# One order for all engines of the wide SwiGLU, worked out in the source; h^T copied back to SBUF; four of eight K pairs of gate and up summed

## The chip, the cores and the metric

The kernel runs on one core of a Trainium2 chip. The metric is the device time of one execution in microseconds, as a median of runs. The core has TensorE (PE, its weight loads shown apart as PEld), VectorE (DVE), ScalarE (ACT), GpSimd (POOL) and SyncE (SP), each with an instruction queue of its own that is worked off in order.

## The reference

One layer of an encoder for 256 tokens of width 2048: two attention branches with a common output projection, a cross-attention, then a SwiGLU feed-forward network, and a last normalization. All is float32. The change touches the feed-forward network (FFN_HIDDEN is 5632):

```python
hf = rms_norm(x, g_ffn[layer])
x = x + (jax.nn.silu(hf @ w_gate[layer]) * (hf @ w_up[layer])) @ w_down[layer]
```

and, in the order of the matmuls alone, the output projection of the attention (w_out).

## The kernel before

**Products.** TensorE works in fp32r, so each operand is split into a high and a low part, and each product is three matmuls (`mm`, L99 to L101): activations high by weights high, high by low, low by high. The activations (names ending in _h, _l, 128x128) are the stationary side, the weights (wh, wl, 512 columns) the moving one. `split_into` makes the parts: ACT casts the high one (L107), DVE subtracts it from the source for the low one (L108). Weights come from DRAM raw (wraw, three buffers of 128x2048, one DMA for each on SP's queue), and are split into four buffers of wh and wl.

**Stages of the FFN.** 5632 hidden columns are one narrow chunk of 512 (`narrow_chunk`, weights w_gate0 and w_up0, input x2T) and five wide ones of 1024 (`wide_chunk`, input xn). While the narrow chunk runs, `normalized_pairs` makes xn: x2T_f is multiplied by the row of 1/rms (rrow), and split. A wide chunk is a projection by gate, a silu on ACT, a projection by up, the product h = u g on DVE, and the transposes of h (`pt`, L502) for w_down. The narrow chunk and the first wide one make the first group, the other four two groups of two. Behind each group, its part of w_down is added to x_res (`wide_add`) in two halves of 1024 columns; the accumulators start from x_res, copied in by ACT (L261).

**Pairs.** The 2048 rows of a projection's weights are 8 K pairs of 256. A plain pair (P) takes 8 products, 24 matmuls. A summed one (W) takes 7 products in the manner of Strassen and Winograd, 21 matmuls, for which DVE makes sums of the weights (`tsum`, L287 to L292) and, once for each activation pair, sums of the activations (`sums`, L245 to L248, and their split, `forms`). The W pairs of a projection gather four of their products in the accumulators q1, q5, q7 and q6; `leave` (L332 to L336) turns these into four partial results on ACT and DVE, and `join` (L340) adds the accumulators of the plain products. `GU_KINDS` gives the kind of each pair, `G_ORDER` and `U_ORDER` the order in which gate and up take them; `DN_KINDS` and `groups` do so for w_down.

**What sets the order.** In the kernel before, the order of the instructions on each engine comes from the scheduler of the language: the code is written stage by stage, and the scheduler interleaves what stands open, by its own estimate. The buffers (three of wraw, four of wh and wl, eight PSUM banks, in two pools that change roles from one projection to the next) bound how far one engine runs ahead.

Of the kernel before, what the change touches and what calls it, by code (L numbers as in the profile page):

```python
# [11 lines left out]
F32 = mybir.dt.float32  # L12
# [26 lines left out]
GU_KINDS = "PPWPWPWP"  # L39

G_ORDER, U_ORDER = (0, 1, 2, 3, 4, 5, 6, 7), (0, 2, 1, 4, 3, 6, 5, 7)
# [13 lines left out]
class Split:  # L55
# [25 lines left out]
def encoder_block(ctx: ExitStack, tc: tile.TileContext, a, out):  # L81
# [15 lines left out]
    def mm(o, l, r, start, stop, seeded=False):  # L97

        nc.tensor.matmul(o, l.h, r.h, start=start, stop=False, skip_group_check=seeded)  # L99
        nc.tensor.matmul(o, l.h, r.l, start=False, stop=False, skip_group_check=seeded)  # L100
        nc.tensor.matmul(o, l.l, r.h, start=False, stop=stop, skip_group_check=seeded)  # L101

# [151 lines left out]
    def wide_project(pairs, src, order, kinds, leave, join, closed=(0, 1), before=None, seed=None):  # L254
# [10 lines left out]
        for n, i in enumerate(order):  # L265
# [4 lines left out]
            if i not in summed:  # L270
                w = [split_blocks(raw[:, 2 * k:2 * k + 2, :]) for k in range(2)]
                for tt in range(NT):
                    for oc in range(2):
                        for k in range(2):

                            ends = stop or i == plain[-1] and tt == oc == 1
                            mm(accs[tt][oc], pairs[i].at(k, tt), w[k][:, oc, :], not used[tt][oc],
                               ends and k == 1 and oc in closed, seed is not None)
                            used[tt][oc] = True
                continue  # L280
# [44 lines left out]
    def wide_result(pairs, src, order, kinds):  # L325
# [16 lines left out]
        wide_project(pairs, src, order, kinds, leave, join)  # L342
# [558 lines left out]
    def wide_chunk(c, kinds):  # L901

        g = wide_result(xn, a["w_gate"][c], G_ORDER, GU_KINDS)
        for tt in range(NT):
            for oc in range(2):
                nc.scalar.activation(g[tt][:, oc, :], g[tt][:, oc, :], AF.Silu)
        u = wide_result(xn, a["w_up"][c], U_ORDER, GU_KINDS)
        t = act_tile(name="hT")
        spare = None
        if kinds[2] == "P":  # L910
            spare = Split(*[wsum.tile([P, 2, S], F32R, name="hT2" + x, tag="hT2" + x, bufs=1) for x in "hl"])
        pts = []
        for oc in range(2):
            for tt in range(NT):
                h = u[tt][:, oc, :]
                nc.vector.tensor_tensor(out=h, in0=h, in1=g[tt][:, oc, :], op=ALU.mult)
                if oc == 0:
                    transposed(t, h, tt, 4)
                    continue
                pt = ps_tile("pt")  # L920
                for j in range(4):
                    nc.tensor.transpose(out=pt[:, j * P:(j + 1) * P], in_=h[:, j * P:(j + 1) * P], identity=ident)  # L922
                pts.append(pt.rearrange("p (j t) -> p j t", t=P))
                if spare:
# [165 lines left out]
```

## Time and profile before

| | |
|---|---|
| median of 3 runs | 1142.08 us (1141.88 to 1142.27) |
| the profiled execution's own time | 1141.65 us |
| its span in the profile | 1139.8 us |
| TensorE busy | 1130.6 us, 5390 matmuls |
| DVE busy | 973.2 us, 1322 instructions |
| ACT busy | 667.5 us, 965 instructions |
| DMA | 222.13 MB, mean 195 GB/s |

The profile is of one execution. Busy times are of each engine by itself; a busy TensorE is not one at its peak. A row of the timeline has the start, the duration, the engine, the line and operation, out<-in by the program's names, shapes, the count of like instructions in a row, and in brackets the idle time ahead with what ended it. Durations of neighbours overlap, since the engines are pipelined, so the cost of one instruction in a row of like ones is the distance of the starts. The rows themselves stand in the prediction, where they are used.

### The profile page before, as it was taken

The numbers are of one execution on the slowest core, as the hardware profiler recorded it, in microseconds if no ns is written. First come the engines' busy times: TensorE is split into PE (matmuls) and PEld (weight loads), VectorE is DVE, ScalarE is ACT, GpSimd is POOL, SyncE is SP. The second block draws the span as 40 slices with busy tenths as digits, with TensorE's granted clock in tenths as the row PEclk, the third lists the DMA queues.
The fourth block names the chain that finished last, engine by engine and source line by source line (L and its number), as shares of the span: only waits on it lengthen the run. The fifth ranks groups of instructions, "written<-read, shape, count | busy, mean of one in ns | idle before, by whom it ended". The sixth has DMA issues, their size and how long they took to land.

```text
span 1139.8 us, 14403 instructions
## 1 busy us (share of the span) xinstructions
PE 1130.6 (99%) x5390; PEld 946.4 (83%) x5390; DVE 973.2 (85%) x1322; ACT 667.5 (59%) x965; POOL 58.6 (5%) x75
## 2 busy tenths in 40 slices
PE   9999999999999999999999999999999999999997
PEld 7888888888788888888888888888888888888886
DVE  7788766878896777989898988998998898999895
ACT  7755455567566555665565555565554564665663
POOL 5910000000001000000000000000000000000000
PEclk9999999999999999999999999999999999999999
DMA  9655333546567444455556556556555555565553
GB/s 362 241 195 185 124 125 139 181 149 224 191 227 259 156 161 179 161 211 189 212 194 219 185 191 218 185 190 216 185 187 220 201 205 190 191 247 196 195 181 129
DMA packets 35494, 222.13 MB, mean 195 GB/s; under 512 B 4321, under 2 KB 5601, under 8 KB 11105
## 3 DMA queue, kind: packets, MB, share of 16 engines
q1 hardware_dynamic: 33696, 216.60, 52.9%
q0 software_dynamic: 864, 3.15, 0.8%
q10 hardware_dynamic: 864, 1.47, 0.4%
q8 instruction: 42, 0.69, 0.2%
q14 instruction: 28, 0.22, 0.1%
HBM read 219.11 MB, written 2.10 MB: 194 GB/s over the span
## 4 chain that ended last, share of the span: by engine, by line
PE 98%; issue 1%; ACT 0%; DVE 0%; POOLq 0%; POOL 0%; ACTq 0%
PE acc L99 26%; PE acc L101 26%; PE acc L100 26%; PE q L100 4%; PE q L99 4%; PE q L101 4%; PE pt L502 2%; PE ppt L650 1%; PE psc L100 1%; PE psc L101 1%; PE psc L99 1%; PE acckv L99 0%; PE acckv L101 0%; PE acckv L100 0%; PE pt L922 0%
## 5 line engine op out<-in xcount | busy, mean ns | idle before, releaser
L107 ACT CAST wh<-wraw 128x1024 fp32r<-128x1024 f32 (+2 forms) x401 | 389.8, 989 | 283.2 <-PE acc L101 219.5
L108 DVE TENSOR_TENSOR wl<-wraw,wh 128x1024 fp32r<-128x1024 f32 (+2 forms) x401 | 455.3, 1148 | 88.8 <-ACT wh L107 86.8
L107 ACT CAST wh<-tsum 128x1024 fp32r<-128x1024 f32 (+1 forms) x98 | 98.0, 1006 | 73.1 <-PE acc L101 29.7
L108 DVE TENSOR_TENSOR wl<-tsum,wh 128x1024 fp32r<-128x1024 f32 (+1 forms) x98 | 113.6, 1165 | 19.5 <-ACT wh L107 19.5
L100 PE MATMUL acc<-wl,x2n_h 128*128 128x512 f32 x320 | 124.5, 390 | 0.0
L101 PE MATMUL acc<-wh,x2n_l 128*128 128x512 f32 x320 | 123.9, 389 | 0.0
L99 PE MATMUL acc<-wh,x2n_h 128*128 128x512 f32 x320 | 108.2, 390 | 0.0
L100 PE MATMUL acc<-wl,x0T_h 128*128 128x512 f32 x224 | 88.5, 395 | 0.0
L101 PE MATMUL acc<-wh,x0T_l 128*128 128x512 f32 x224 | 88.2, 394 | 0.0
L99 PE MATMUL acc<-wh,x0T_h 128*128 128x512 f32 x224 | 86.9, 396 | 0.0
L100 PE MATMUL q<-wl,forms_h 128*128 128x512 f32 x191 | 74.3, 389 | 0.0
L101 PE MATMUL q<-wh,forms_l 128*128 128x512 f32 x191 | 74.1, 389 | 0.0
L100 PE MATMUL acc<-wl,hT_h 128*128 128x512 f32 x188 | 73.3, 392 | 0.0
L101 PE MATMUL acc<-wh,hT_l 128*128 128x512 f32 x188 | 72.4, 389 | 0.0
L101 PEld LDWEIGHTS acc<-wh,x2n_l 128*128 128x128 f32 x320 | 60.1, 188 | 12.4
L100 PEld LDWEIGHTS acc<-wl,x2n_h 128*128 128x128 f32 x320 | 60.1, 188 | 12.3
L99 PEld LDWEIGHTS acc<-wh,x2n_h 128*128 128x128 f32 x320 | 59.9, 188 | 12.3
L99 PE MATMUL q<-wh,forms_h 128*128 128x512 f32 x191 | 66.7, 389 | 0.0
L99 PE MATMUL acc<-wh,hT_h 128*128 128x512 f32 x188 | 64.5, 391 | 0.0
L100 PE MATMUL acc<-wl,forms_h 128*128 128x512 f32 x162 | 62.5, 389 | 0.0
L101 PE MATMUL acc<-wh,forms_l 128*128 128x512 f32 x162 | 62.4, 389 | 0.0
L99 PE MATMUL acc<-wh,forms_h 128*128 128x512 f32 x162 | 61.3, 389 | 0.0
(402 smaller groups left out, 2247.9 us busy)
## 6 DMA issues: line engine op xcount, KB each, us to landing
wraw<-in_w_gate SPq DMA_DIRECT2D x44, 1024.0 KB, 4.8
wraw<-in_w_up SPq DMA_DIRECT2D x44, 1024.0 KB, 4.8
wraw<-in_w_dn SPq DMA_DIRECT2D x41, 1024.0 KB, 4.8
wraw<-in_w_in SPq DMA_DIRECT2D x24, 1024.0 KB, 4.8
wraw<-in_w_out SPq DMA_DIRECT2D x16, 1024.0 KB, 4.8
wraw<-in_w_in_lat SPq DMA_DIRECT2D x5, 832.0 KB, 7.2
wraw<-in_w_xk SPq DMA_DIRECT2D x4, 1024.0 KB, 5.4
wraw<-in_w_xq SPq DMA_DIRECT2D x4, 1024.0 KB, 5.9
```

The source lines that it names most:

```text
L99: nc.tensor.matmul(o, l.h, r.h, start=start, stop=False, skip_group_check=seeded)
L100: nc.tensor.matmul(o, l.h, r.l, start=False, stop=False, skip_group_check=seeded)
L101: nc.tensor.matmul(o, l.l, r.h, start=False, stop=stop, skip_group_check=seeded)
L107: last_cast[0] = nc.scalar.copy(out=dst.h, in_=src).ins
L108: last_split[0] = nc.vector.tensor_tensor(out=dst.l, in0=src, in1=dst.h.bitcast(F32), op=ALU.subtract).ins
L502: nc.tensor.transpose(out=pt[:, j * P:(j + 1) * P], in_=src[:, j * P:(j + 1) * P], identity=ident)
L650: nc.tensor.transpose(out=pt[:, kt * S + tt * P:kt * S + (tt + 1) * P], in_=p[:, tt, kt * P:(kt + 1) * P], identity=ident)
```

## The change

The wide chunks and all w_down stages behind them are no longer written for the language's scheduler. The new code describes every instruction as an operation with its engine, a duration from a table (`V_COLS`, `S_COLS`, `PASS`), what it needs, and which buffers it takes and gives back (`Ring`, `Hold`). `Flow.emit` fixes TensorE's order as the source has it, works out when each operation is wanted by that order, simulates the engines, and issues the operations in the order found: of those that are open on an engine the one that is wanted first. It runs inside a block in which the language's scheduler keeps the given order.

With it come four edits. `GU_KINDS` has one more W pair (four of eight), and gate and up take the pairs in one order, (0, 2, 1, 4, 3, 6, 7, 5). In the products of a weight block the two matmuls on wh stand first and those on wl last (`mm_late`, `on_tensor`), in the projection by w_out too. The transposed h is copied back from PSUM to SBUF by ACT into the place of u, and splits, sums and forms read it there; the separate copy `a21` of before goes. The pairs of w_down are taken in another order.

The parameters `by_transfer` and `carried` and the function `wide_result`, which the diff touches, are not used by the code after. The diff, cut to its core:

```diff
-GU_KINDS = "PPWPWPWP"
-G_ORDER, U_ORDER = (0, 1, 2, 3, 4, 5, 6, 7), (0, 2, 1, 4, 3, 6, 5, 7)
+GU_KINDS = "PPWPWPWW"
+G_ORDER = U_ORDER = (0, 2, 1, 4, 3, 6, 7, 5)
+V_COLS, S_COLS = {1024: (1.136, 1.218), 512: (0.602, 0.684), 256: (0.336, 0.416), 128: (0.202, 0.282)}, \
+    {1024: (0.954, 1.053), 512: (0.523, 0.621), 256: (0.265, 0.368)}
+PASS, PASS_LAG, TURN, LOADED = 0.2267, 0.2, 0.108, (4.8, 2.75)
...
+        t = 0.0
+        for o in self.chains["PE"]:
+            o.wanted, t = t, t + o.busy
...
+        for o in reversed(sorted_ops):
+            for n, data in o.then:
+                o.wanted = min(o.wanted, n.wanted - (o.lag + self.HANDOVER if data else 0.0))
...
+        for _ in self.ops:
+            picked = None
+            for engine, ops in open_ops.items():
+                if not ops:
+                    continue
+                f = free.get(engine, 0.0)
+                soon = min(max(f, o.ready) for o in ops) + self.CHOICE
+                o = min((o for o in ops if max(f, o.ready) <= soon), key=lambda o: (o.wanted, place[o]))
+                start = max(f, o.ready)
+                if picked is None or start < picked[0]:
+                    picked = start, o
...
+            o.fn()
...
+    def mm_late(products, seeded=False):
+        for o, l, r, start, stop in products:
+            nc.tensor.matmul(o, l.h, r.h, start=start, stop=False, skip_group_check=seeded)
+            nc.tensor.matmul(o, l.l, r.h, start=False, stop=False, skip_group_check=seeded)
+        for o, l, r, start, stop in products:
+            nc.tensor.matmul(o, l.h, r.l, start=False, stop=stop, skip_group_check=seeded)
...
+    def on_split(cols, src, dst, tiles, need, take, give):
+        def high():
+            tiles()
+            nc.scalar.copy(out=dst().h, in_=src())
+        def low():
+            last_split[0] = nc.vector.tensor_tensor(out=dst().l, in0=src(), in1=dst().h.bitcast(F32),
+                                                    op=ALU.subtract).ins
+        h = on_scalar(cols, high, need=need, take=take, give=give)
+        return h, on_vector(cols, low, need=[h], give=give)
...
+            s13 = on_vector(1024, sums, need=[loaded], take=[t_hold], give=[raw_hold])
+            s2 = on_vector(512, lambda more=more: more(2), need=[s13])
+            s4 = on_vector(512, lambda more=more: more(3), need=[s2], give=[raw_hold])
...
+            parts = (((q(1), A11, 0, *own), (acc(0, 1), S3, 1, False, last)), ((q(5), S5, 0, *own), (q(7), S7, 1, *own)),
+                     ((acc(0, 0), A12, 0, False, last),), ((q(6), S6, 0, *own), (acc(1, 0), A22, 1, False, last)))
...
+            for m, (part, (nb, block, need, give, ring)) in enumerate(zip(parts, blocks)):
+                w, hold, h, l = flow_weights(got, nb, block, [need], [give], ring)
+                products = [(o, a, w(j), st, sp) for o, a, j, st, sp in part]
+                opens = own[0] and m == 0
+                on_tensor(products, False, [h] + ready, q_holds.values() if opens else [], [hold], seeded,
+                          open_q if opens else None)
+                done = on_tensor(products, True, [l], (), [hold], seeded)
+            if own[1]:
+                left = leave(Q, q_holds, done)
+        banks.reverse()
+        joined = {(tt, oc): join(tt, oc, acc(tt, oc), holds[tt, oc], [done, left]) for tt, oc in holds if oc in closed}
...
-    def wide_chunk(c, kinds):
-        g = wide_result(xn, a["w_gate"][c], G_ORDER, GU_KINDS)
-        for tt in range(NT):
-            for oc in range(2):
-                nc.scalar.activation(g[tt][:, oc, :], g[tt][:, oc, :], AF.Silu)
-        u = wide_result(xn, a["w_up"][c], U_ORDER, GU_KINDS)
...
+    def flow_chunk(c, kinds):
+        g_unit, u_unit = unit(), unit()
+        g, g_hold, g_joined = flow_result(a["w_gate"][c], G_ORDER, g_unit)
+        def silu(tt, oc):
...
+        u, u_hold, u_joined = flow_result(a["w_up"][c], U_ORDER, u_unit)
+        pool = banks[1]
+        back = {}
         for oc in range(2):
             for tt in range(NT):
...
+                m = on_vector(512, times, need=[g_done[tt, oc], u_joined[tt, oc]], give=[g_hold])
+                o = flow.op("PE", 4 * TURN, 4 * TURN + 0.25, turn, need=[m], take=[hold])
+                back[tt, oc] = flow.op("S", 0.484, 0.589, lambda tt=tt, oc=oc, pt=pt: nc.scalar.copy(
+                    out=u(tt, oc), in_=pt[0]), need=[o], give=[hold])
...
-    groups = [([0], (0, 1, 2, 4, 5, 3)), ([1, 2], (0, 1, 2, 4, 3, 6, 7, 5)), ([3, 4], (0, 1, 2, 4, 3, 6, 7, 5))]
+    groups = [([0], (0, 1, 4, 2, 5, 3)), ([1, 2], (0, 1, 2, 4, 5, 3, 7, 6)), ([3, 4], (0, 1, 2, 4, 5, 3, 7, 6))]
...
         for c in chunks:
-            hp += wide_chunk(c, DN_KINDS[pair0 + len(hp):])
+            pairs, m, ring = flow_chunk(c, DN_KINDS[pair0 + len(hp):])
+            hp += [lambda n=n, pairs=pairs: pairs[n] for n in range(4)]
+            made += m
+            used += ring
...
+                done = flow_add(hp, made, src[h], order, kinds, 2 * h)[2]
...
+        flow_add(hp, made, src[0], order, kinds, 0, final_square)
+        accs, join = flow_add(hp, made, src[1], (0, 2, 1, 3, 4), DN_LAST[-8:], 2, closed=(1,))[:2]
+        with tc.manual_schedule():
+            flow.emit({"PE": 10.0})
```

**The seam between the narrow chunk and the first wide one, on TensorE.** acc_4564 is the last accumulator of up0 before (acc_4573 after); x2n are the plain pairs of xn, so matmuls with x2n_h and x2n_l are those of the first gate projection; pt takes the transposes of the narrow chunk's h, of its first and second 128 tokens. Before:

```order
L100 MATMUL acc_4564<-wl_4674,x2T_h_4321 128x512
L101 MATMUL acc_4564<-wh_4673,x2T_l_4322 128x512
L100 MATMUL acc_4725<-wl_4732,x2n_h_4508 128x512
L101 MATMUL acc_4725<-wh_4731,x2n_l_4509 128x512
L99 MATMUL acc_4725<-wh_4735,x2n_h_4508 128x512
L100 MATMUL acc_4725<-wl_4736,x2n_h_4508 128x512
L101 MATMUL acc_4725<-wh_4735,x2n_l_4509 128x512
L99 MATMUL acc_4725<-wh_4765,x2n_h_4508 128x512
L100 MATMUL acc_4725<-wl_4766,x2n_h_4508 128x512
L101 MATMUL acc_4725<-wh_4765,x2n_l_4509 128x512
L99 MATMUL acc_4725<-wh_4769,x2n_h_4508 128x512
L502 MATMUL pt_4707<-ident_104,h_4705 128x128 x4
```

The same place after:

```order
L201 MATMUL acc_4573<-wl_4683,x2T_h_4321 128x512
L202 MATMUL acc_4573<-wh_4682,x2T_l_4322 128x512
L1041 MATMUL acc_4762<-wh_4742,x2n_h_4508 128x512
L1042 MATMUL acc_4762<-wh_4742,x2n_l_4509 128x512
L616 MATMUL pt_4716<-ident_104,h_4714 128x128 x4
L1041 MATMUL acc_4763<-wh_4742,x2n_h_4508 128x512
L1042 MATMUL acc_4763<-wh_4742,x2n_l_4509 128x512
L616 MATMUL pt_4727<-ident_104,h_4725 128x128 x4
L1041 MATMUL acc_4764<-wh_4742,x2n_h_4508 128x512
L1042 MATMUL acc_4764<-wh_4742,x2n_l_4509 128x512
```

Nine matmuls of the gate projection stood between up0 and the first transposes, and now two (two more, into acc_4761, stand within up0). The second transposes came 26 matmuls behind the first, and now two.

**The same seam on DVE.** wl are the low parts of weights, forms_l those of the activations' forms, sums the activations' sums, tsum the sums of weights, h the narrow chunk's product of silu and up. Before:

```order
L108 TENSOR_TENSOR wl_4732<-wraw_4729,wh_4731 128x1024
L248 TENSOR_TENSOR sums_4516<-x2T_f_4201,sums_4516 128x128
L248 TENSOR_TENSOR sums_4533<-x2T_f_4262,sums_4533 128x128
L108 TENSOR_TENSOR wl_4736<-wraw_4729,wh_4735 128x1024
L248 TENSOR_TENSOR sums_4548<-x2T_f_4323,sums_4548 128x128
L108 TENSOR_TENSOR wl_4766<-wraw_4763,wh_4765 128x1024
L108 TENSOR_TENSOR forms_l_4515<-sums_4516,forms_h_4514 128x512
L897 SCALAR_TENSOR_TENSOR h_4705<-acc_4563,x2Tr_4348,sg_4703 128x512
L108 TENSOR_TENSOR forms_l_4532<-sums_4533,forms_h_4531 128x512
L108 TENSOR_TENSOR forms_l_4547<-sums_4548,forms_h_4546 128x512
```

After:

```order
L1053 TENSOR_TENSOR wl_4746<-wraw_4736,wh_4745 128x1024
L1131 TENSOR_TENSOR tsum_4753<-wraw_4738 128x1024
L217 TENSOR_TENSOR forms_l_4515<-sums_4516,forms_h_4514 128x512
L1053 TENSOR_TENSOR wl_4751<-wraw_4738,wh_4750 128x1024
L217 TENSOR_TENSOR forms_l_4532<-sums_4533,forms_h_4531 128x512
L217 TENSOR_TENSOR forms_l_4547<-sums_4548,forms_h_4546 128x512
L217 TENSOR_TENSOR forms_l_4560<-sums_4561,forms_h_4559 128x512
L1136 TENSOR_TENSOR tsum_4753<-tsum_4753,wraw_4738 128x512
L1011 SCALAR_TENSOR_TENSOR h_4714<-acc_4572,x2Tr_4348,sg_4712 128x512
L1053 TENSOR_TENSOR wl_4759<-tsum_4753,wh_4758 128x1024
L1011 SCALAR_TENSOR_TENSOR h_4725<-acc_4573,x2Tr_4348,sg_4723 128x512
```

Four pairs of forms are made where three were, and all four, with two sums of weights, now stand ahead of the first h; before, one stood ahead of it. Counted from the multiplication of x2T_f by rrow, four of 1024 columns, to the first h, DVE's queue had 11 instructions of 1024 columns, 6 of 512, 6 of 256 and 12 of 128, and now has 12, 9, 8 and 16.

**From gate to up within a wide chunk, on DVE.** res are the results of gate, L340 before and L1203 after the joins; wl2 the low part of the last two sums of a W pair. Before:

```order
L340 TENSOR_TENSOR res0_4998<-acc_4725,res0_4998 128x512
L292 TENSOR_TENSOR tsum_5095<-tsum_5095,wraw_5085 128x512
L335 TENSOR_TENSOR res1_4999<-res1_4999,q7_4801 128x512
L340 TENSOR_TENSOR res0_4998<-acc_4726,res0_4998 128x512
L108 TENSOR_TENSOR wl_5098<-tsum_5095,wh_5097 128x1024
L336 TENSOR_TENSOR res1_4999<-q5_4800,res1_4999 128x512
L108 TENSOR_TENSOR wl2_5108<-tsum_5095,wh2_5107 128x1024
L108 TENSOR_TENSOR wl_5102<-wraw_5085,wh_5101 128x512
L340 TENSOR_TENSOR res1_4999<-acc_4727,res1_4999 128x512
L340 TENSOR_TENSOR res1_4999<-acc_4728,res1_4999 128x512
```

After:

```order
L1131 TENSOR_TENSOR tsum_5074<-wraw_5000 128x1024
L1203 TENSOR_TENSOR res0_5049<-acc_4761,res0_5049 128x512
L1203 TENSOR_TENSOR res0_5049<-acc_4762,res0_5049 128x512
L1203 TENSOR_TENSOR res1_5050<-acc_4763,res1_5050 128x512
L1203 TENSOR_TENSOR res1_5050<-acc_4764,res1_5050 128x512
L1053 TENSOR_TENSOR wl_5070<-wraw_5000,wh_5069 128x1024
L1136 TENSOR_TENSOR tsum_5074<-tsum_5074,wraw_5000 128x512
L1053 TENSOR_TENSOR wl_5094<-tsum_5074,wh_5093 128x1024
L1136 TENSOR_TENSOR tsum_5074<-tsum_5074,wraw_5000 128x512
L1053 TENSOR_TENSOR wl_5116<-wraw_5000,wh_5115 128x512
L1053 TENSOR_TENSOR wl_5135<-wraw_5036,wh_5134 128x1024
L1053 TENSOR_TENSOR wl2_5141<-tsum_5074,wh2_5140 128x1024
```

The joins stood among the splits of up's first W pair; now all four stand in one block ahead of them, and the splits follow in the order in which TensorE takes them.

More of the change, by code (lines that the diff above doesn't have):

```diff
@@ L62, in __getitem__, with __init__ @@
         return Split(self.h[idx], self.l[idx])
+class Ring:
+    def __init__(self, n):
+        self.n, self.holds = n, []
+class Hold:
+    def __init__(self, ring):
+        self.gives = []
+        before = ring.holds[-ring.n] if len(ring.holds) >= ring.n else None
+        self.after = before.gives if before else []
+        ring.holds.append(self)
+class Op:
+    def __init__(self, engine, busy, lag, fn, need, take, transfer):
+        self.engine, self.busy, self.lag, self.fn, self.transfer = engine, busy, lag, fn, transfer
+        self.need, self.take = [n for n in need if n is not None], take
+        self.before, self.then, self.wanted, self.ready, self.left = [], [], 1e9, 0.0, 0
@@ new lines, in encoder_block, with unit, on_vector, on_scalar @@
+    rings = {"raw": Ring(3), "w": Ring(4), "t": Ring(1), "w2": Ring(1), "sums": Ring(1), "left": Ring(1), "odd": Ring(1)}
+    psum = {id(pacc): Ring(4), id(pps): Ring(4)}
+    units = [Ring(1) for _ in range(5)]
+    x_done = {}
+    def unit():
+        return units.pop(0)
+    def on_vector(cols, fn, **deps):
+        return flow.op("V", *V_COLS[cols], fn, **deps)
+    def on_scalar(cols, fn, **deps):
+        return flow.op("S", *S_COLS[cols], fn, **deps)
+    def on_tensor(products, late, need, take=(), give=(), seeded=False, tiles=None):
+        n = len(products) * (1 if late else 2)
+        def fn():
+            if tiles is not None:
+                tiles()
+            for o, l, r, start, stop in products:
+                o, l, r = o(), l(), r()
+                if late:
+                    nc.tensor.matmul(o, l.h, r.l, start=False, stop=stop, skip_group_check=seeded)
+                else:
+                    nc.tensor.matmul(o, l.h, r.h, start=start, stop=False, skip_group_check=seeded)
+                    nc.tensor.matmul(o, l.l, r.h, start=False, stop=False, skip_group_check=seeded)
+        return flow.op("PE", n * PASS, n * PASS + PASS_LAG, fn, need=need, take=take, give=give, chain="PE")
@@ new lines, in flow_chunk, with tiles @@
+        t_hold = Hold(t_unit)
+        need = None
+        for tt in range(NT):
+            def tiles(tt=tt):
+                if tt == 0:
+                    t[0] = act_tile(name="hT")
+            h, l = on_split(512, lambda tt=tt: turned(tt, 0), lambda tt=tt: t[0][:, :, tt * P:(tt + 1) * P], tiles,
+                            [back[tt, 0], need], [t_hold] if tt == 0 else [], [u_hold])
+            made.append(l)
+            need = h
+        both = flow.op("none", 0.0, 0.0, lambda: pairs.update({0: Pair(t[0][:, 0:2, :]), 1: Pair(t[0][:, 2:4, :])}),
+                       need=made)
```

320 lines of the change are left out of this document (274 added, 46 removed).

## The prediction

> **What bounds the kernel now.** I read the page first (busy shares, slices, chain), then the chain of waits in order of time, then windows cut at the stages of the FFN, then the timeline at the places where the change moves work.
>
> ```profile
> span 1139.8 us, 14403 instructions
> PE 1130.6 (99%) x5390; PEld 946.4 (83%) x5390; DVE 973.2 (85%) x1322; ACT 667.5 (59%) x965; POOL 58.6 (5%) x75
> PE   9999999999999999999999999999999999999997
> ...
> PE 98%; issue 1%; ACT 0%; DVE 0%; POOLq 0%; POOL 0%; ACTq 0%
> ...
> L107 ACT CAST wh<-wraw 128x1024 fp32r<-128x1024 f32 (+2 forms) x401 | 389.8, 989 | 283.2 <-PE acc L101 219.5
> L108 DVE TENSOR_TENSOR wl<-wraw,wh 128x1024 fp32r<-128x1024 f32 (+2 forms) x401 | 455.3, 1148 | 88.8 <-ACT wh L107 86.8
> ```
>
> TensorE is busy in every slice and is 98% of the chain. ACT's casts of the weights wait for TensorE (219.5 us in which a buffer had to come free) and DVE waits for ACT (86.8 us): the converters run ahead and are held back. Only two things can move the end: the number of matmuls, and new waits of TensorE. One matmul of 512 columns costs, by the chain in order of time,
>
> ```profile
> 917.17 1.13 PE acc L99 x5
> ```
>
> 1.13 / 5 = 0.2267 us. The windows of the first wide gate/up chunk, a later one, and the w_down stages behind the first and the second group:
>
> ```profile
> 480.00:567.00 87.00, 87.00 (x392) 72.03 (x391) 78.56 (x89) 49.54 (x58) 0.00 (x0) 1.00 0.55 196
> 567.00:630.00 63.00, 63.00 (x284) 52.21 (x283) 58.61 (x76) 36.65 (x47) 0.00 (x0) 1.00 0.55 201
> 714.00:799.00 85.00, 85.00 (x384) 70.48 (x384) 79.68 (x99) 51.27 (x65) 0.00 (x0) 1.00 0.56 198
> 799.00:882.00 83.00, 83.00 (x376) 68.83 (x375) 74.67 (x88) 46.72 (x57) 0.00 (x0) 1.00 0.56 203
> ```
>
> (Columns: window, length, busy time and count of PE, PEld, DVE, ACT, POOL, then the granted clock, DMA share, GB/s.) TensorE has no gap in any of them, at clock 1.00. DVE is busy 78.56 of 87 and 79.68 of 85 us in a chunk; its reserve there is small, and the change spends DVE time. That is what has to be priced.
>
> **The change, part by part.** *Fewer matmuls.* A pair of kind P is 24 matmuls, one of kind W 21 (7 products by 3). Gate and up of five wide chunks are 10 projections, and one more pair of each becomes W: 30 matmuls less, and 30 x 0.2267 = **6.8 us off TensorE**. It counts in full where the stage stays gapless. No wait of TensorE in the FFN is there to be removed, so a better order by itself gains nothing, and 6.8 us is the most that can be gained.
>
> *Free edits.* The new order of the three matmuls of a product (the two on wh first, the one on wl last) changes no count: there is one weight load for each matmul already (x5390 of both), 83% busy beside them. The copy of h^T back by ACT adds 20 copies of 512 columns and drops eight small ones; ACT is at 59% and waits 283 us ahead of its casts, and the result is wanted only in the w_down stage. SP and POOL issue the same transfers in the same order, at a DMA share of 0.55. The other down orders change no count. If the cover of ACT were gone, its casts would be late at DVE first, which is the slower rival below.
>
> *The seam between the narrow chunk and the first wide one.* Here the order shown above puts more DVE work ahead of the narrow chunk's h, while TensorE's transposes of h stand earlier among the matmuls. Rows of before, DVE:
>
> ```profile
> 463.00:473.00 10.00, 10.00 (x46) 8.20 (x45) 10.00 (x24) 7.76 (x12) 0.00 (x0) 1.00 0.31 107
> 473.00:484.00 11.00, 11.00 (x52) 9.08 (x51) 11.00 (x16) 4.90 (x8) 0.00 (x0) 1.00 0.56 202
> ...
> 457.66 4.62 DVE L868 TENSOR_TENSOR x2T_f<-x2T_f,rrow 128x1024 f32<-128x1024 f32 x4
> ...
> 468.16 0.75 DVE L108 TENSOR_TENSOR forms_l<-x2T_f,forms_h 128x256 fp32r<-128x256 f32 x2
> 468.83 0.68 DVE L108 TENSOR_TENSOR x2n_l<-x2T_f,x2n_h 128x512 fp32r<-128x512 f32 x1
> 469.43 0.28 DVE L246 TENSOR_TENSOR sums<-x2T_f,sums 128x128 f32<-128x128 f32 x1
> 469.64 0.75 DVE L108 TENSOR_TENSOR forms_l<-x2T_f,forms_h 128x256 fp32r<-128x256 f32 x2
> ...
> 477.60 0.68 DVE L108 TENSOR_TENSOR forms_l<-sums,forms_h 128x512 fp32r<-128x512 f32 x1
> 478.20 0.74 DVE L897 SCALAR_TENSOR_TENSOR h<-acc,x2Tr,sg 128x512 f32<-128x512 f32 x1
> 478.86 1.28 DVE L108 TENSOR_TENSOR forms_l<-sums,forms_h 128x512 fp32r<-128x512 f32 x2
> 480.06 1.22 DVE L287 TENSOR_TENSOR tsum<-wraw 128x1024 f32<-128x1024 f32 x1
> 481.20 1.22 DVE L108 TENSOR_TENSOR wl<-wraw,wh 128x1024 fp32r<-128x1024 f32 x1
> 482.33 0.74 DVE L897 SCALAR_TENSOR_TENSOR h<-acc,x2Tr,sg 128x512 f32<-128x512 f32 x1
> ```
>
> DVE is busy without a gap here (10.00 of 10, 11.00 of 11), so what stands ahead of the first h counts in full. From start to start: 1.135 us for 1024 columns (480.06 to 482.33, two), 0.60 for 512 (477.60 to 478.20), 0.335 for 256 (468.16 to 468.83, two), 0.20 for 128 (469.43 to 469.64). Between the multiplication by rrow (457.66) and the first h, the order of before has 11 of 1024 columns, 6 of 512, 6 of 256 and 12 of 128: 12.49 + 3.60 + 2.01 + 2.40 = 20.50 us by these durations, and the trace has 478.20 - 457.66 = 20.54. The same count for after is 12 of 1024, 9 of 512, 8 of 256 and 16 of 128: 13.62 + 5.40 + 2.68 + 3.20 = 24.90. So the first h starts **4.4 us later**, at 482.6, and is done at about 483.4. TensorE:
>
> ```profile
> 477.28 0.39 PE L101 MATMUL acc<-wh,x2T_l 128*128 128x512 f32 x1
> 477.50 0.39 PE L100 MATMUL acc<-wl,x2n_h 128*128 128x512 f32 x1
> ...
> 479.55 0.60 PE L502 MATMUL pt<-ident,h 128*128 128x128 f32 x4
> 479.91 0.48 PE L99 MATMUL acc<-wh,x2n_h 128*128 128x512 f32 x1
> 480.22 0.40 PE L100 MATMUL acc<-wl,x2n_h 128*128 128x512 f32 x1
> ...
> 485.94 0.60 PE L502 MATMUL pt<-ident,h 128*128 128x128 f32 x4
> ...
> 478.72 0.68 ACT L895 ACTIVATE sg<-acc,x2Tr 128x512 f32<-128x512 f32 x1
> ```
>
> Before, the first transposes stand nine matmuls behind the last of up0, at 479.55, just after h was done. After, two matmuls of the new stage stand between up0 and the transposes (and two within up0): TensorE reaches them at 477.50 + 4 x 0.2267 = 478.4 and **waits 5.0 us**, and everything in its queue waits with it. Then come two matmuls and the second transposes, whose h is a weight split (1.14) and an h (0.66) behind the first on DVE; the four transposes (479.55 to 480.22 less one matmul: 0.45) and two matmuls (0.45) take 0.9 of those 1.8 us, so TensorE waits some 0.8 more. Sum **5.8 us**; 5.1 to 6.5 if DVE's 25 us run 3% faster or slower than counted. ACT's second silu of gate0, which the second h needs too, stood at 478.72 and is not what ends either wait. Behind it DVE is 4 to 5 us ahead of TensorE and no further wait follows.
>
> *The clock at that wait.*
>
> ```profile
> 1.17 4.24 PE L384 MATMUL wps<-warm 128*128 128x512 bf16 x11 [1.17 <-DVE warm L378]
> ...
> 1131.00:1133.00 2.00, 1.78 (x15) 1.58 (x14) 1.43 (x6) 0.48 (x1) 0.00 (x0) 1.00 0.84 305
> 1133.00:1135.50 2.50, 0.00 (x0) 0.00 (x0) 1.80 (x6) 1.06 (x2) 0.55 (x1) 1.00 0.47 176
> 1135.50:1139.00 3.50, 0.00 (x0) 0.00 (x0) 0.21 (x1) 0.27 (x1) 0.00 (x0) 0.50 0.81 300
> ```
>
> At the end of the kernel TensorE stops at 1132.8 and the granted clock is 0.50 from 1135.5, 2.7 us later. At the start eleven matmuls (eight of 512 columns and three of 256, 9.5 in units of 512) take 4.24 us, 0.446 each: half speed for some 4.2 us. No row shows an idle stretch of 5 us in mid-kernel, so its cost has two bounds: nothing (the clock stays), and 3.4 us (half speed for 6.8 us, to the end of a second period of the length between idle and full that the start shows). I take the row of the start: 4.2 us at half speed lose 2.1, of which 0.8 falls into the second wait that is there anyway: **+1.3 us**. The Trainium skill ("TensorE: Matmul & The Clock Gate", Part 1: The HAM clock gate) speaks for less: it says that the clock halves after a whole idle window of about 3.4 us on a free-running grid. A fall 2.7 us after the last matmul, shorter than a window, doesn't agree with it. By that rule the wait of 5.0 us would hold a whole window in about (5.0 - 3.4) / 3.4, half of the cases, and the term would be 0.65.
>
> *The other seams.* Between gate and up of a chunk (the second place shown in the order), DVE has, behind gate's last matmul: 0.3 us handover, four joins of 512 columns (2.4), the split of 1024 (1.14), a sum (0.6), a split (1.14), a sum (0.6), a split of 512 (0.6), two splits of 1024 (2.28): 9.1 us until the last sums of up's first W pair are split. TensorE has 24 matmuls of the plain pair and 19 of the W pair ahead of the one that takes them: 43 x 0.2267 = 9.75 us. **Slack 0.6 us**, five times in the kernel. Counted alike, the seam from up to the next gate has 0.6 and that to w_down 1.5. I cost these at nothing; with the cover gone it is the slower rival.
>
> *Sum.* -6.8 + 5.8 + 1.3 = **+0.3 us** on the profiled execution's 1141.65, so 1141.95. The median of the runs, 1142.08, is 0.43 above that execution: **1142.4**.
>
> **Rivals.** *The wait comes, the clock stays.* -6.8 + 5.8 = -1.0: 1142.08 - 1.0 = 1141.1. For it: the idle stretch that cost clock in the rows is the kernel's end, where nothing follows; it decides where the 5.0 us fall against the clock's own periods, which the trace can't tell in advance. The rule named above makes about half of the cases of it.
>
> *The whole gain lands.* 1142.1 - 6.8 = 1135.3. It needs the first h done when TensorE comes to it, which needs DVE 4.4 us further on. DVE's one gap nearby:
>
> ```profile
> 453.00:463.00 10.00, 10.00 (x47) 8.24 (x46) 7.71 (x7) 6.68 (x11) 0.00 (x0) 1.00 0.59 211
> ```
>
> holds 2.3 us and lies ahead of 457.66, while all added work but the sums of the weights (1.7 us) needs the product with rrow. Against it, then; for it only that I may have misread what is queued where.
>
> *DVE becomes the bound of the wide chunks (slower).* A W pair in place of a P pair adds to DVE four instructions of 1024 columns and three of 512 for two of 1024: 2 x 1.135 + 3 x 0.60 = 4.1 us, 8.2 us a chunk, and takes 6 x 0.2267 = 1.4 us from TensorE. From the windows above: 78.56 + 8.2 = 86.8 against 87 - 1.4 = 85.6, and 79.68 + 8.2 = 87.9 against 83.6: over by 1.2 and 4.3 us, some 2.7 in the mean. In the w_down stages DVE has 4.4 (58.61 of 63) and 8.3 us (74.67 of 83) free. So DVE must run ahead before a pair of chunks, or leave h's work over to w_down; the buffers (three of raw weights, four of split ones) bound how far. It decides at the seam from gate to up: once the joins are over 0.6 us late, TensorE waits there, and each further chunk adds its overrun. Of the two pairs of chunks I let the second chunk of each pay in full: 2 x 2.7 = 5.4, and 1142.4 + 5.4 = **1147.8**; all five chunks would be 13.5.
>
> **How the numbers follow.** Chances: wait and slow clock (the forecast) 0.36, wait alone 0.22, whole gain 0.20, DVE as the bound 0.22. The forecast's own range is 1140.4 (no clock term, a wait of 5.1) to 1145.2 (a wait of 6.5 and 3.4 for the clock). The range reaches to the centres of the outer cases, 1135.0 to 1148.0, with about 0.1 left out at either side. A measurement can tell 0.2% (2.3 us) from no change: faster is below 1139.8, slower above 1144.4. Faster: the whole gain and a fifth of the second case, 0.25. Slower: nearly all of the last case and a tenth of the forecast, 0.24. Within: 0.51.
>
> **What would show it.** Right: 30 matmuls less; one idle stretch of TensorE of 5 us about 478 us, ended by DVE's first h, with a shorter one behind it; the granted clock under 1 in the window behind it; chunk windows about 1.4 us shorter without a gap. Wrong: the first h of the narrow chunk within 478 to 480 us (the order doesn't mean what I read in it), or TensorE idle at the start of up, ended by a DVE split (the slack of 0.6 us was not there), or a chunk of 86 us and more with DVE gapless. Wrong too if TensorE's pace in the chunks isn't 0.2267 with the new order of the three matmuls.

## The result and the profile after

| | before | after |
|---|---|---|
| median | 1141.90 us (1141.55 to 1142.45) | 1144.96 us (1143.88 to 1145.67) |
| ratio after to before | | 1.0026, interval 1.0018 to 1.0034 |
| span of the profiled execution | 1139.8 us | 1142.5 us |
| matmuls | 5390 | 5360 |

The change made the kernel 3.1 us slower. The predicted 1142.4 was 2.6 us too low. The time lies in the range given, but above the 1144.4 from which the prediction called the kernel slower, with a chance of 0.24. The page of after, its busy times, slices of TensorE and DVE, and chain, and last the slices of DVE before:

```profile
span 1142.5 us, 14716 instructions
PE 1127.7 (99%) x5360; PEld 941.6 (82%) x5360; DVE 1014.8 (89%) x1378; ACT 694.6 (61%) x999; POOL 56.4 (5%) x75
PE   9999999999999999899999999999999999999997
DVE  7788766878896776999999999999999999999995
PE 84%; DVE 11%; issue 3%; ACT 1%; DMA 1%; POOLq 0%; POOL 0%; SPq 0%; DVEq 0%; ACTq 0%
...
DVE  7788766878896777989898988998998898999895
```

Thirty matmuls are gone. From the 17th slice (457 us) on, DVE was at tenths of 8 and 9 and is now at 9 in every slice but the last, and it holds 11% of the chain where it held none: TensorE has come to wait for it. The five largest waits of TensorE in after, in total, number and longest:

```profile
PE acc L1041 <- ACT sg L1009: 2.8, 1, 2.8
PE wps L498 <- DVE warm L492: 1.2, 1, 1.2
PE pt L616 <- DVE h L1011: 1.0, 1, 1.0
PE q L1039 <- DVE wl L1053: 0.9, 2, 0.6
PE acc L1041 <- ACT wh L1050: 0.7, 1, 0.7
```

A gap between matmuls costs more than the wait shown: in the rows of the seam below, the start behind the wait of 2.82 us comes 2.98 us late, and the next one stands 0.34 behind it. So I add up, from the timeline, the distance of each two starts less 0.2267 us (0.1075 for a transpose). By that count, in us:

| kernel | w_out (250 to 300 us) | seam at 465 to 492 us | from 492 us to the end of w_down |
|---|---|---|---|
| before | 1.47 | 0.16 | 0.54 |
| after | 0.24 | 6.88 | 4.23 |

So 30 x 0.2267 = 6.8 us of matmuls and 1.2 in w_out were gained, 6.7 were lost at the seam and 3.7 behind it: together 2.4 of the 2.7 us by which the span grew. (The medians are 3.1 apart: the profiled execution of after, 1144.28, lies 0.7 under its median, that of before 0.25 under its own. What made the other runs of after longer no trace shows.) Nearly all of the 3.7 lies late in the first half of each w_down stage and, 1.5 of it, at the start of the last half.

**The seam, TensorE and then DVE and ACT of after:**

```profile
477.50 0.39 PE L202 MATMUL acc<-wh,x2T_l 128*128 128x512 f32 x1
480.71 0.50 PE L1041 MATMUL acc<-wh,x2n_h 128*128 128x512 f32 x1 [2.82 <-ACT sg L1009]
481.05 0.40 PE L1042 MATMUL acc<-wh,x2n_l 128*128 128x512 f32 x1
482.46 1.11 PE L616 MATMUL pt<-ident,h 128*128 128x128 f32 x4 [1.02 <-DVE h L1011]
483.23 0.78 PE L1041 MATMUL acc<-wh,x2n_h 128*128 128x512 f32 x1
...
456.70 4.62 DVE L982 TENSOR_TENSOR x2T_f<-x2T_f,rrow 128x1024 f32<-128x1024 f32 x4
481.66 0.74 DVE L1011 SCALAR_TENSOR_TENSOR h<-acc,x2Tr,sg 128x512 f32<-128x512 f32 x1
483.46 0.74 DVE L1011 SCALAR_TENSOR_TENSOR h<-acc,x2Tr,sg 128x512 f32<-128x512 f32 x1
...
479.97 0.69 ACT L1009 ACTIVATE sg<-acc,x2Tr 128x512 f32<-128x512 f32 x1 [0.96 <-DVE forms_l L217]
```

The first h starts 481.66 - 456.70 = 24.96 us behind the product with rrow; the count from the order gave 24.9. But the first thing that stops TensorE isn't h. It is a matmul of the first gate projection, which waits 2.8 us for the second silu (sg) of the narrow chunk. That silu reads the gate accumulator whose PSUM bank this matmul needs, and it is itself late for a buffer: sums, silu and h share five of them, four W pairs hold four, and one comes free with forms_l. Behind it TensorE waits for the first h. From the end of up0 (477.73) to the first h's transposes it had two matmuls to run, and two more to the second's. A wait of 0.7 us for a weight cast, already within up0, comes on top.

**The stage behind the second group.** TensorE at its wait, and DVE's windows in the first 26 and 35 us of the w_down stages behind the first and the third group:

```profile
833.32 0.40 PE L1042 MATMUL acc<-wh,forms_l 128*128 128x512 f32 x1
833.84 0.50 PE L1039 MATMUL q<-wl,forms_h 128*128 128x512 f32 x1
...
563.00:589.00 26.00, 26.00 (x125) 21.70 (x124) 25.66 (x41) 17.20 (x26) 0.00 (x0) 1.00 0.46 165
1045.00:1080.00 35.00, 35.00 (x164) 29.26 (x163) 34.93 (x55) 22.23 (x31) 0.00 (x0) 1.00 0.51 180
```

(The third busy time is DVE's.) DVE has no gap there: 25.66 of 26 us and 34.93 of 35, and 35.93 of 36 behind the second group (below). It enters the stage with the transposed h of the last chunk still to be split and summed, and meets the stage's own summed pairs. TensorE then stands waiting for the last split of a summed pair: q<-wl starts 0.52 us behind the matmul ahead of it at 833.84, 0.3 late, and in the stage behind the first group it waits 0.6 us. The first 36 us and the rest of the stage behind the second group, before and then after:

```profile
799.00:835.00 36.00, 36.00 (x169) 29.88 (x168) 32.80 (x41) 21.90 (x31) 0.00 (x0) 1.00 0.56 198
835.00:882.00 47.00, 47.00 (x209) 38.95 (x208) 41.88 (x48) 24.82 (x27) 0.00 (x0) 1.00 0.57 207
...
794.00:830.00 36.00, 36.00 (x168) 30.07 (x167) 35.93 (x56) 22.86 (x32) 0.00 (x0) 1.00 0.49 175
830.00:877.00 47.00, 46.88 (x205) 38.17 (x204) 44.63 (x50) 28.35 (x32) 0.00 (x0) 1.00 0.57 208
```

Before, DVE had 3.2 us free in the first part and 5.1 in the rest; after, nothing and 2.4.

### The profile page after: what moved, and what is told of

The parts are those of the page before. It is cut to its first block, busy times and chain, and to the rows that moved or that the text cites. A ratio compares the mean times of both kernels' runs of the same rounds, so it can differ in the third digit from the quotient of the medians.

```text
span 1142.5 us, 14716 instructions
## 1 busy us (share of the span) xinstructions
PE 1127.7 (99%) x5360; PEld 941.6 (82%) x5360; DVE 1014.8 (89%) x1378; ACT 694.6 (61%) x999; POOL 56.4 (5%) x75
## 3 DMA queue, kind: packets, MB, share of 16 engines
q10 hardware_dynamic: 864, 1.47, 0.4%
## 4 chain that ended last, share of the span: by engine, by line
PE 84%; DVE 11%; issue 3%; ACT 1%; DMA 1%; POOLq 0%; POOL 0%; SPq 0%; DVEq 0%; ACTq 0%
PE acc L1042 11%; PE acc L1041 11%; PE acc L1039 11%; PE acc L200 8%; PE acc L201 8%; PE acc L202 8%; DVE wl L1053 4%; PE q L1039 3%; PE q L1042 3%; PE q L1041 3%; PE acc L207 2%; PE acc L208 2%; PE acc L210 2%; PE pt L616 1%; DVE tsum L1136 1%
## 5 line engine op out<-in xcount | busy, mean ns | idle before, releaser
L1050 ACT CAST wh<-wraw 128x1024 fp32r<-128x1024 f32 x242 | 228.2, 957 | 95.4 <-PE acc L1042 64.5
L1053 DVE TENSOR_TENSOR wl<-wraw,wh 128x1024 fp32r<-128x1024 f32 x242 | 261.1, 1100 | 5.6 <-ACT wh L1050 3.5
L217 DVE TENSOR_TENSOR wl<-wraw,wh 128x1024 fp32r<-128x1024 f32 (+3 forms) x159 | 187.0, 1187 | 57.4 <-ACT wh L216 54.7
L216 ACT CAST wh<-wraw 128x1024 fp32r<-128x1024 f32 (+3 forms) x159 | 158.9, 1012 | 118.3 <-PE acc L202 76.0
L1050 ACT CAST wh<-tsum 128x1024 fp32r<-128x1024 f32 x108 | 113.7, 1054 | 114.1 <-DVE tsum L1131 51.4
L1053 DVE TENSOR_TENSOR wl<-tsum,wh 128x1024 fp32r<-128x1024 f32 x108 | 131.7, 1220 | 6.0 <-ACT wh L1050 5.4
L1041 PE MATMUL acc<-wh,x2n_h 128*128 128x512 f32 x320 | 125.6, 392 | 3.5 <-ACT sg L1009 2.8
L1039 PE MATMUL acc<-wl,x2n_h 128*128 128x512 f32 x320 | 85.8, 390 | 0.0
L1041 PE MATMUL q<-wh,forms_h 128*128 128x512 f32 x216 | 84.5, 391 | 0.3 <-ACT wh L1050 0.3
L1136 DVE TENSOR_TENSOR tsum<-tsum,wraw 128x512 f32<-128x512 f32 x108 | 74.0, 686 | 0.5
```

The lines of the kernel that those rows point to most:

```text
L216: last_cast[0] = nc.scalar.copy(out=dst.h, in_=src).ins
L217: last_split[0] = nc.vector.tensor_tensor(out=dst.l, in0=src, in1=dst.h.bitcast(F32), op=ALU.subtract).ins
L1039: nc.tensor.matmul(o, l.h, r.l, start=False, stop=stop, skip_group_check=seeded)
L1050: nc.scalar.copy(out=dst().h, in_=src())
L1053: last_split[0] = nc.vector.tensor_tensor(out=dst().l, in0=src(), in1=dst().h.bitcast(F32), op=ALU.subtract).ins
L1136: nc.vector.tensor_tensor(out=t[:, j, :], in0=t[:, 0 if j == 2 else 2, :], in1=got["raw"][:, j, :], op=ALU.add)
```

## Experiments

Each is a change to the kernel after, unless said otherwise. All medians stand beside a median of before of 1142.0 to 1142.2 from the same chip.

**1. Other banks for the first gate projection.**

```diff
         ua = project(x2T, [a["w_up0"][0, i] for i in range(4)])
+        banks.reverse()
```

> The narrow chunk's accumulators and the first gate projection's share one PSUM pool; here the two pools change roles behind up0, so the first gate projection finds four free banks, and by the order 24 of its matmuls stand ahead of the first transposes of h instead of 4. DVE's work ahead of the first h is unchanged (24.9 us by the count). Theory (TensorE waits because it has nothing it may run until the narrow chunk's h frees its banks and is transposed): the seam's loss falls from 6.7 us to about 1.3 (a wait of 0.6 for the second h and some 0.7 for a weight cast early), the granted clock stays at 1.00 there, the median is about 1139.6. Rival (the wait only moves: DVE, as late as before, is next late with the splits of the first W pair): the seam keeps 3 us or more, the median is 1142 or above.

Measured: 1140.31 us, ratio to before 0.9985 (0.9976 to 0.9993). The seam of this kernel, TensorE and DVE:

```profile
478.85 0.39 PE L202 MATMUL acc<-wh,x2T_l 128*128 128x512 f32 x1
479.08 1.07 PE L1040 MATMUL acc<-wl,x2n_h 128*128 128x512 f32 x4
...
482.72 0.60 PE L616 MATMUL pt<-ident,h 128*128 128x128 f32 x4
484.22 0.66 PE L616 MATMUL pt<-ident,h 128*128 128x128 f32 x4 [0.90 <-DVE h L1012]
484.63 0.48 PE L1042 MATMUL q<-wh,forms_h 128*128 128x512 f32 x1
...
481.61 0.76 DVE L1012 SCALAR_TENSOR_TENSOR h<-acc,x2Tr,sg 128x512 f32<-128x512 f32 x1
483.40 0.76 DVE L1012 SCALAR_TENSOR_TENSOR h<-acc,x2Tr,sg 128x512 f32<-128x512 f32 x1
```

DVE's h comes at 481.61, as late as in after (481.66), yet TensorE runs without a gap until 483.0. What is left is 1.1 us for the second h and 0.8 for an early weight cast: the seam's loss is 2.2 instead of 6.9, and the median falls by 4.65. So a late h isn't the whole cause. It costs that much because the new order of the matmuls opens four accumulators in turn, where the old one filled them one after the other, and three of their four banks still belonged to the narrow chunk. The rival (the wait moves on to the first W pair) fell.

**2. A sixth buffer for sums, silu and h.**

```diff
-    nat_pool[:] = wsum, 5
+    nat_pool[:] = wsum, 6
```

> Six buffers of 128x512 in place of five for sums, silu and h of the narrow chunk, so the second silu need not wait for DVE's forms. By the order the first h comes 1.8 us sooner on DVE (23.1 us behind the product with rrow instead of 24.9), and TensorE's order is unchanged. Theory (DVE's queue ahead of h sets the end of the wait; the silu's wait lay inside it): TensorE's wait for the silu (2.8 us) goes, the wait for the first h takes its place, and only 1.8 us are won: median about 1143.2, or 1141.5 if the clock stays at 1.00. Rival (the silu's buffer, and the bank it holds, are the cause): 3.0 us of wait and 1.7 of clock go, median about 1140.3.

Measured: 1144.48 us, 1.0021 of before (1.0012 to 1.0030): 0.5 less than after. TensorE at the seam, and the two h on DVE:

```profile
479.18 0.50 PE L1041 MATMUL acc<-wh,x2n_h 128*128 128x512 f32 x1 [1.77 <-ACT sg L1009]
480.20 1.11 PE L616 MATMUL pt<-ident,h 128*128 128x128 f32 x4 [0.28 <-DVE h L1011]
483.80 1.11 PE L616 MATMUL pt<-ident,h 128*128 128x128 f32 x4 [1.63 <-DVE h L1011]
...
479.38 0.76 DVE L1011 SCALAR_TENSOR_TENSOR h<-acc,x2Tr,sg 128x512 f32<-128x512 f32 x1
482.98 0.76 DVE L1011 SCALAR_TENSOR_TENSOR h<-acc,x2Tr,sg 128x512 f32<-128x512 f32 x1
```

Neither expectation held. The first h came 1.8 us sooner, but the work that stood ahead of it now stands ahead of the second, which came no sooner against the rest (up0 ended 0.48 us earlier in this execution, the second h 0.48). Much of the wait went from the silu and the first h to the second, and in this execution the clock was low for two periods instead of one. The median hides two groups. In five of the eleven runs the mean granted clock is 0.998 or 0.999, as in before, and they take 1143.3 to 1143.6 us; in six it is 0.995 to 0.997, and they take 1144.5 to 1146.1. All 13 runs of after have 0.995 or 0.996. So whether the clock falls at the seam differs here from run to run, and the 0.5 us say little. The silu's buffer was no cause by itself: the end of the seam is set by the second h.

**3. The order of w_down as before.**

```diff
-    groups = [([0], (0, 1, 4, 2, 5, 3)), ([1, 2], (0, 1, 2, 4, 5, 3, 7, 6)), ([3, 4], (0, 1, 2, 4, 5, 3, 7, 6))]
+    groups = [([0], (0, 1, 4, 2, 5, 3)), ([1, 2], (0, 1, 2, 4, 3, 6, 7, 5)), ([3, 4], (0, 1, 2, 4, 3, 6, 7, 5))]
```

> The w_down stages behind the two pairs of chunks take the pairs in the order of before (0,1,2,4,3,6,7,5), with a plain pair between the second and the third summed pair; all else as after. Theory (DVE needs 6.3 us for a summed pair and TensorE 4.8, so two in a row run DVE's lead down): the waits near 832 and 1083 us go, together about 2.4 us, median about 1142.6. Rival (the lateness is work left over from the chunks): the waits only move to another summed pair, median 1144.5 to 1145.5.

Measured: 1146.64 us, 1.0041 (1.0028 to 1.0054), 1.7 slower than after. The theory fell: with the summed pairs apart, the one taken fifth waits longer. That the wait moves to another summed pair is what the rival said, but the time lies above its 1145.5.

```profile
PE q L1039 <- DVE wl L1053: 3.4, 5, 1.1
```

It was 0.9 us in two waits in after. Two summed pairs in a row are not the trouble, an early one is.

**4. Three summed pairs in gate and up.**

```diff
-GU_KINDS = "PPWPWPWW"
+GU_KINDS = "PPWPWPWP"
```

> The change with three summed pairs of eight in gate and up, as before; order, copies and everything else as after. 30 matmuls more: +6.8 us. Theory (the fourth pair's DVE time makes both the waits of w_down, 4.0 us, and half of the seam): the w_down waits go, the first h comes 3.3 us sooner (21.6 us behind the product with rrow), the seam's loss falls from 6.7 to about 3: median about 1144.2. Rival (the waits come from the new order, not from the fourth pair): all waits stay, median about 1151.5.

Measured: 1145.04 us, 1.0034 (1.0021 to 1.0048); the theory had 1144.2, its rival 1151.5. Behind the seam 0.15 us are left of 4.2, so that part of the theory held. The seam loses 4.8 and not 3: the first h starts 21.7 us behind the product with rrow, only 1.1 later than in before, and still TensorE, with so few matmuls ahead of the transposes, waits 2.3 and 2.0 us for the two h. (Three runs lie at 1144.8 to 1145.0, two, with the clock at 0.996 against 0.998 and 0.999, at 1147.0 and 1147.2.) With 30 matmuls more the kernel takes the same time as after: the fourth pair's 6.8 us were spent on its own waits.

**5. Exchanged banks, and plain pairs first in w_down.**

```diff
-    groups = [([0], (0, 1, 4, 2, 5, 3)), ([1, 2], (0, 1, 2, 4, 5, 3, 7, 6)), ([3, 4], (0, 1, 2, 4, 5, 3, 7, 6))]
+    groups = [([0], (0, 1, 2, 3, 4, 5)), ([1, 2], (0, 1, 4, 5, 2, 6, 3, 7)), ([3, 4], (0, 1, 4, 5, 2, 6, 3, 7))]
```

> As the kernel with the exchanged banks (1140.31), with w_down taking its plain pairs first: (0,1,2,3,4,5) behind the first chunk and (0,1,4,5,2,6,3,7) behind the pairs of chunks. DVE has no idle time in the first 30 us of each w_down stage (35.97 of 36 us behind the second group). Theory (DVE enters the stage with work left over from the chunks and needs plain pairs, 2.3 us of DVE against 5.4 of TensorE, before summed ones, 6.3 against 4.8): the waits near 588, 829 and 1080 us go, together 2.1 us, and the 1.2 us near 1096 may; median 1137 to 1138.3. Rival (DVE's whole load in the stage is too large whatever the order): the waits move to the end of the half, where three summed pairs stand close together; median 1140 or above.

Measured: 1167.85 us, 1.0226 (1.0212 to 1.0240). The theory fell; the rival (1140 or above, with the waits at the end of the half) named the place, but by far not the size. The largest waits of TensorE:

```profile
PE acc L1042 <- ACT acc L1101: 11.0, 6, 3.1
PE q L1043 <- DVE forms_l L1054: 4.8, 3, 2.1
PE acc L1042 <- DVE left L1183: 3.4, 4, 1.0
```

With the summed pairs at the end, the four q accumulators are read out (left) only when the half is over, and the next half's accumulators, started by ACT from x (L1101), need the same banks. The last chunk's forms are late too. The granted clock was 0.5 for 13.7 us in mid-kernel, which costs at most another 6.8. This reading goes by the waits alone; no run separates its parts. "Late enough for DVE" and "early enough for the banks" stand against each other here.

**6. Exchanged banks, and one summed pair fewer in the first half of each w_down stage.**

```diff
+DN_FIRST = "PP" + "PPWP" + ("PPWW" + "PPPP") * (NPC // 2)
-        flow_add(hp, made, src[0], order, kinds, 0, final_square)
+        flow_add(hp, made, src[0], order, first, 0, final_square)
```

(and the same kinds for the first halves behind the other groups and in the layout of w_down)

> As the kernel with the exchanged banks, with one summed pair fewer in the first half of each w_down stage (pair 5 of the first, pair 7 of the others are plain there): 9 matmuls more, +2.0 us, and 4.1 us less for DVE in each. Theory (DVE's load in those 30 us is the cause of the waits): the waits of w_down, 3.3 us in all, go, median about 1139.0. Rival (they come from the order in which DVE takes its work, not from its load): they stay, median about 1142.4.

Measured: 1138.23 us, **0.9966 of before (0.9954 to 0.9979)**. The theory held, and 0.8 us more: TensorE has no wait left behind the seam (0.4 us by the count, before has 0.5). The largest waits, and then the first 36 us of the stage behind the second group:

```profile
PE wps L500 <- DVE warm L494: 1.2, 1, 1.2
PE pt L618 <- DVE h L1014: 0.9, 1, 0.9
PE acc L1044 <- ACT wh L1053: 0.7, 1, 0.7
...
789.00:825.00 36.00, 36.00 (x169) 30.05 (x168) 35.90 (x57) 24.18 (x34) 0.00 (x0) 1.00 0.49 175
```

DVE is as gapless there (35.90 of 36 us) as in after, and TensorE loses nothing. A DVE without a gap is thus not yet a wait; what counts is whether a split is done when TensorE comes to it.

**7. Exchanged banks, and three summed pairs in up alone.**

```diff
+UP_KINDS = "PPWPWPWP"
-        u, u_hold, u_joined = flow_result(a["w_up"][c], U_ORDER, u_unit)
+        u, u_hold, u_joined = flow_result(a["w_up"][c], U_ORDER, u_unit, UP_KINDS)
```

> As the kernel with the exchanged banks, with three summed pairs in up and four in gate: 15 matmuls more, +3.4 us, and 4.1 us less for DVE in each chunk. Theory (the load that the fourth pair adds is carried out of the chunks into w_down): half of it removed is enough, since DVE then has 84 us of work for some 84 us of TensorE; the waits of w_down go, 3.6 us: median about 1140.1. Rival (w_down's own load makes the waits): they stay, median about 1143.7.

Measured: 1139.24 us, 0.9976 (0.9967 to 0.9985), with 0.5 us lost behind the seam. DVE time taken out of the chunks ends the waits of w_down as well as DVE time taken out of w_down: they are one account.

**8. The kernel before with the new kinds and order of gate and up alone.**

```diff
-GU_KINDS = "PPWPWPWP"
+GU_KINDS = "PPWPWPWW"
-G_ORDER, U_ORDER = (0, 1, 2, 3, 4, 5, 6, 7), (0, 2, 1, 4, 3, 6, 5, 7)
+G_ORDER = U_ORDER = (0, 2, 1, 4, 3, 6, 7, 5)
```

> The kernel before with the new kinds and the new order of gate and up alone (four summed pairs), everything else, the language's scheduler among it, as before: 30 matmuls less, -6.8 us. It takes one accumulator after the other, so one free bank lets TensorE run on at the seam. Theory (the seam's loss comes from the four accumulators at once, and the fourth pair by itself costs only DVE time): the seam loses 2.5 us or less, w_down 3 to 4: median 1138 to 1142. Rival (without the order laid out in the source DVE is late at many places): median 1144 or above.

Measured: 1171.52 us, 1.0258 (1.0244 to 1.0272); the rival was right, and by far. The first h starts 24.96 us behind the product with rrow, as late as in after, and the seam loses 3.3 us with one accumulator filled after the other, where after loses 6.9; but 34 us are lost behind it, in more than thirty waits from 513 us on, most of them for casts and splits of weights. Its DVE is busy 1014.7 us, that of after 1014.8: the same work, in another order. What the change does beside the fourth pair is worth the 27 us between the two. I take the laid-out order to be most of it, but that isn't shown: its parts were not run one by one but for w_out and the pairs of w_down.

**9. w_out in its old order of matmuls.** The projection by w_out as in before, the FFN as in after.

```diff
-                            products.append((accs[tt][oc], pairs[i].at(k, tt), w[k][:, oc, :], not used[tt][oc],
-                                             ends and k == 1 and oc in closed))
+                            mm(accs[tt][oc], pairs[i].at(k, tt), w[k][:, oc, :], not used[tt][oc],
+                               ends and k == 1 and oc in closed, seed is not None)
...
-                    mm_late(products, seed is not None)
```

> The change with the projection by w_out in the order of before (the three matmuls of a product together, one accumulator after the other); the FFN as after. In the trace of before TensorE loses 1.2 us in w_out to a wait for the copy of x into an accumulator (0.75 us and the restart), in that of after nothing. Theory (the new order of w_out's matmuls took that wait away): it is back, median about 1146.1. Rival (the wait depends on something else that varies from run to run): median about 1145.0, without the wait in the trace.

Measured: 1146.50 us, 1.0039 (1.0026 to 1.0051), 1.5 above after, with the wait back:

```profile
289.27 0.50 PE L200 MATMUL acc<-wh,mixT_h 128*128 128x512 f32 x1 [0.74 <-ACT acc L375]
```

**10. Kernel 6 with six buffers.** Both edits, 2 and 6.

> The best kernel so far (exchanged banks and one summed pair fewer in the first half of each w_down stage, 1138.23) with six buffers for sums, silu and h. By the order the first h comes 1.2 us sooner on DVE, and the second as late as before, since the work that stood ahead of the first now stands between the two. Theory (what is left of the seam is the wait for the second h, 1.1 us): nothing changes, median about 1138.2. Rival (the first h, or the silu's buffer, holds TensorE there): median about 1137.1.

Measured: 1138.12 us, 0.9966 (0.9952 to 0.9979): no change, as the theory said. What is left of the seam is the wait for the second h and the one for the weight cast.

## Why the prediction missed by 2.6 us

**Fewer matmuls, -6.8 us:** right; 30 are gone, and TensorE's pace in the chunks stayed at 0.2267.

**"No wait of TensorE in the FFN is there to be removed ... 6.8 us is the most that can be gained":** wrong by 1.2 us, outside the FFN. I named the new order of matmuls in w_out free of cost and didn't look for a wait there that it could end. The trace of before has one, for a copy of x into an accumulator; run 9 brings it back.

**The seam, 5.8 + 1.3 = 7.1 us:** 6.7 measured, and that the two sums agree so well is in part luck. DVE's delay was right to 0.1 us. (In the sum, 1.8 less 0.9 is 0.9, where I took 0.8.) The picture of TensorE was incomplete: I had it run up to the transposes and wait there in order. It stopped two matmuls earlier, for a bank held by a late silu, so that "is not what ends either wait" was wrong of the silu. By the count the seam's 6.9 us are some 1.0 for a weight cast that I didn't foresee, 3.1 for the silu, 1.2 for the first h, nothing for the second, and 1.7 with the clock at half. Run 1 shows that with free banks the same late h costs 1.1 us. The order's rows showed four accumulators opened in turn, and I counted instructions there and not banks. The clock fell as forecast, for 3.41 us where I had 4.2.

**"I cost these at nothing":** the step that failed. DVE's surplus in the chunks was seen and priced (1.2 to 4.3 us a chunk), and the rival has the right mechanism, but I looked for its end at the seam from gate to up, where after has no wait. The w_down stages were credited with 4.4 and 8.3 us of DVE time to spare. These are totals of a stage, and the splits of the first half's last summed pair are wanted before its end: of the 8.3, only 3.2 lie in the first 36 us, and the surplus that arrives there fills them (35.93 of 36). In the last stage the lateness goes on into the second half. The 3.7 us lost so are the term that is missing in the sum: +0.3 - 1.2 - 0.4 + 3.7 = +2.4, the 2.4 that the count of the spans gives. Runs 4, 6 and 7 take DVE's load away in three ways (and give TensorE 30, 9 and 15 matmuls more), and the waits go with it each time; run 3 shows that the order alone can make them larger.

**The other orders of w_down:** "change no count" was right and beside the point; they are worth 1.7 us (run 3).

Left open: the 0.8 us that a matmul of the gate projection waits within up0 for a weight cast, in after and in kernel 6 alike, and whether an order of DVE in which the second h comes before the splits that stand ahead of it would end the wait of 1.1 us. Neither was tried.

## What to carry to other kernels

Where an order of matmuls opens several accumulators at once, count the banks that are free at that moment, and not only the instructions: the same late vector result cost 1.1 us where the matrix engine had other banks to work in, and most of 6.9 where it had none. The reserve of an engine that is busy nine tenths counts only up to the moment at which its next result is wanted: of 8.3 us in a stage, 3.2 came in time. And a saving on the bound engine that is paid for on the next one can be taken too far: here nine matmuls handed back, three in each w_down stage, cost 2.0 us and brought 4.1 (run 6 against run 1).

## What the runs showed of the hardware

The clock needs no whole idle period to fall. Windows that end and begin where the granted clock changes, of after, of run 2 and of run 8, then two of run 4, in which it stayed, and last the end of before, behind which it fell:

```profile
478.75:482.16 3.41, 0.73 (x2) 0.30 (x2) 3.41 (x6) 0.95 (x2) 0.00 (x0) 1.00 0.50 209
482.16:485.57 3.41, 3.11 (x11) 2.49 (x12) 3.24 (x5) 0.76 (x2) 0.00 (x0) 0.50 0.00 0
```

```profile
476.45:479.86 3.41, 1.64 (x7) 0.76 (x5) 3.41 (x5) 2.58 (x4) 0.00 (x0) 1.00 0.96 338
479.86:483.27 3.41, 2.02 (x7) 1.25 (x6) 3.41 (x6) 0.59 (x1) 0.00 (x0) 0.50 0.10 43
483.27:486.69 3.41, 2.89 (x9) 2.50 (x10) 2.36 (x4) 1.47 (x3) 0.00 (x0) 0.50 0.00 0
```

```profile
725.26:728.67 3.42, 1.67 (x6) 1.07 (x7) 3.42 (x6) 0.25 (x1) 0.00 (x0) 1.00 0.00 0
728.67:732.09 3.41, 3.41 (x14) 2.98 (x13) 3.41 (x5) 1.63 (x2) 0.00 (x0) 0.50 0.85 307
```

```profile
474.86:478.27 3.41, 1.85 (x9) 1.20 (x7) 3.41 (x6) 2.74 (x5) 0.00 (x0) 1.00 1.01 375
478.27:481.68 3.41, 1.58 (x8) 1.06 (x8) 3.41 (x6) 1.32 (x3) 0.00 (x0) 1.00 0.32 135
```

```profile
1132.10:1135.51 3.41, 0.68 (x6) 0.48 (x4) 2.17 (x8) 1.07 (x2) 0.55 (x1) 1.00 0.62 234
```

The clock changes on a grid of 3.41 us: in after it is low for 3.41 us and then full for 651.95, 191 times 3.413. The grid doesn't begin with the kernel; the first change, to full clock, comes 3.8 to 6.8 us behind the start in the twelve traces. The clock fell behind periods in which TensorE was busy 0.73, 1.64 and 1.67 us, so with no gap above 3 us, and stayed behind others with 1.85 and 1.58. The fall 2.7 us behind the last matmul of before, which the prediction found too early for a whole idle period, is one of these: it came at the end of a period with 0.68 us of work. The Trainium skill ("TensorE: Matmul & The Clock Gate", Part 1: The HAM clock gate) has the length and the free-running grid, and here the traces agree; it asks for an idle window, and these were up to half busy. Where the line lies, about half of a period, these rows don't settle, as 1.58 stayed and 1.67 fell.
